# One hybrid decoder layer on one core: the token mixer's state scans, page use, weight splits and softmax scaling rearranged

## The chip, the cores and the metric

The kernel runs on one core of a Trainium2 chip, in one launch. The time is device microseconds (us) of one execution. The kernel before took 987.81 us in the median of three runs (985.87 to 990.09). The profiled execution took 985.9 us, of which 984.1 us are the span that the profile shows.

## The reference, cut to what matters

The input x is 512 tokens by 1024 channels, all float32. The layer is: a SwiGLU feed-forward block (width 2816), a token mixer, a second SwiGLU block, each with an RMS norm before and after it and a residual. The mixer projects the normed x to q, k, v (512 channels each) and u (512 channels), and computes two things that are concatenated and projected back:

```
# attention, 4 heads, two score maps c = 0, 1 a head (64 channels each), causal
p = softmax(q_c k_c^T / 8);  a = p[0] - lam * p[1];  o = rms_norm(a @ v, sub_g) * (1 - lam_init)
# state space, 32 groups of 16 channels, 64 complex states a group
state_t = a_bar * state_(t-1) + b_bar u_t;   y = Re(C state) + D u
g = gelu(y);  out = rms_norm(g * sigmoid(g @ w_glu + b_glu), norm_g)
```

## The kernel before, in words

**Matmul operands.** Almost every matmul is float32 by splitting: an operand is cast to a rounded high part (`wh`, `hi`) by ScalarE (ACT), and the rest (`wl`, `lo`) is the difference, taken by another engine; three products are added in PSUM (`mm3`, L182 to L184). `weights` (L160 to L177) loads 128x1024 values into `raw` (3 buffers), then splits them into `wh`, `wl` (4 buffers each), or into a heap page where `paged` is set. Which engine takes `wl` is the second argument of `split`: GpSimd (POOL) for paged weights, otherwise `lo_engine[0]`, which is VectorE (DVE) in the two feed-forward blocks and POOL from the start of the mixer to the last step of `fill`.

**Memory.** `page` hands out one of 15 heap pages of 128 x 2048 float32; `scratch` one of 6 buffers of 128 x 512; `bank` a PSUM bank by tag: four "acc", two "sc", two "m". A tile that finds no free buffer waits until an earlier one's last reader is done.

**Mixer, first part.** `out_block` of the first feed-forward block runs in two halves of 512 columns. Late in the second half a hook starts the next norm (`Normed`) and loads the four u weights (`ssm_lead`, paged). Then `ssm_load_states` requests the phase table `phases` and the input maps `im` (1 MB each transfer); `ssm_project` computes u (`ps_u`), writes it to DRAM as `ud` and reads it back regrouped as `u` in 16 small-packet transfers; `ssm_load_outputs` requests the output maps `om` and `mm` (2 and 16 transfers). `att_query(0)`, `att_key(0)`, four `ssm_states(blk)` and `att_values` follow.

**`ssm_states`.** For 8 groups a block: 16 fp32 matmuls into an "sc" bank (`ps_s`, L774); DVE multiplies it by cosines and by sines (L782, L783); POOL adds and subtracts (L785, L786); eight DVE scans of 64 steps with a per-partition decay (L791); products with cosines on DVE (L795) and with sines on POOL (L796); four DVE instructions combine them into `xt` (L802, L803), which stays in scratch until `ssm_outputs` reads it (`ps_y`, L813).

**Mixer, second part.** `attention` runs 16 score blocks (4 heads x 4 query tiles) in an order written out by hand for TensorE (PE) (`manual_schedule`); between them `pad` takes pieces of other PE work from `fill`: the q and k projections of heads 1 to 3, `ssm_outputs`, `glu`, the output projection. `att_scores` computes both maps into the two "sc" banks (`ps_sc`, L917 to L919), takes the row maximum on DVE (L921), the exponential with its row sum on ACT (L922), and on DVE the reciprocals times the coefficients (L924, L925), the scaling of map 0 (L926) and the combination (L927). `att_mix` transposes the result, copies it (L936) and multiplies by v (`ps_o`, L943). `att_norm` scales by the RMS norm and by `sub_g` (L954); `rsqrt_of` adds eps on DVE (L192) and takes the power on POOL (L193). `att_out` transposes and splits (L969, L970).

**Order.** Outside `manual_schedule` a planner orders every engine's instructions at build time by program order and by its own costs; on the chip each engine runs its list in that order.

Of the kernel before, what the change touches and what calls it, by code (L numbers as in the profile page):

```python
# [8 lines left out]
F32 = mybir.dt.float32  # L9
# [4 lines left out]
ALU = mybir.AluOpType  # L14
# [27 lines left out]
LO_ATT = 1  # L42
# [7 lines left out]
def hybrid_layer(  # L50
# [100 lines left out]
    lo_engine = [dve]  # L151
# [14 lines left out]
    def weights(src, shape, paged=False, late=None):  # L166
        raw = ring.tile(shape, F32, tag="raw", name="raw", bufs=3)
        if late is not None:
            pool.tensor_copy(raw[:, 0, 0:1], late)
        weights.dma = sp.dma_start(out=raw, in_=src).ins  # L170
        if paged:
            both = page([P, 2] + list(shape[1:]), F32R, "w_lead")
            wh, wl = both[:, 0], both[:, 1]
        else:
            wh = ring.tile(shape, F32R, tag="wh", name="wh")
            wl = ring.tile(shape, F32R, tag="wl", name="wl")
        with after(*behind):  # L177
            split(raw, wh, wl, pool if paged else lo_engine[0])
        return wh, wl
# [552 lines left out]
    def ssm_load_outputs():  # L732
        S.mm, S.om = [], []
        kd = S.kd.rearrange("(g h) s -> h g s", h=CH)
        for j in range(2):
# [16 lines left out]
    def ssm_project(xn, started, lead_w):  # L752
        units = [(bank("acc", "ps_u"), w) for w in lead_w]
        halves(units, xn, started)
        for j, (ps, _) in enumerate(units):
            ut = scratch([P, TC, NC], F32, "ut")
            act.copy(ut, ps.rearrange("p (c t) -> p t c", t=TC))
            act.dma_start(out=ud[j * P:(j + 1) * P, :], in_=ut.rearrange("p t c -> p (t c)"))
        S.u = page([P, GROUPS, NC], F32, "u")
        for hf in range(2):  # L760
            src = ud[hf * 256:(hf + 1) * 256, :].rearrange("(g h) (t c) -> t h g c", h=CH, t=TC)
            for tau in range(TC):
                sp.dma_start(out=S.u[tau * CH:(tau + 1) * CH, hf * 16:hf * 16 + 16, :], in_=src[tau])
        S.g = page([P, 4, SW], F32, "g")
        S.x = {}

    def ssm_states(blk):
# [12 lines left out]
        tcos = scratch([P, 2, 256], F32, "tcos")  # L780
        tsin = scratch([P, 2, 256], F32, "tsin")
        dve.tensor_tensor(tcos, pv, cos, ALU.mult)  # L782
        dve.tensor_tensor(tsin, pv, sin, ALU.mult)  # L783
        z = scratch([P, 2, 256], F32, "z")
        pool.tensor_tensor(z[:, 0], tcos[:, 0], tsin[:, 1], ALU.add)  # L785
        pool.tensor_tensor(z[:, 1], tcos[:, 1], tsin[:, 0], ALU.subtract)  # L786
        w = scratch([P, 2, 256], F32, "w")
        for ri in range(2):
            for g in range(4):
                cs = slice(g * NC, (g + 1) * NC)  # L790
                dve.tensor_tensor_scan(w[:, ri, cs], S.r8[:, blk * 4 + g:blk * 4 + g + 1].broadcast_to([P, NC]),  # L791
                                       z[:, ri, cs], 0.0, ALU.mult, ALU.add)
# [104 lines left out]
    def att_key(h, xn):  # L897

        A.k[h] = k = page([P, 3, SEQ], F32R, "k")
        ps = bank("acc", "ps_k2")  # L900
        yield from col_steps(ps, col_weights(w_in, 512 + h * P), xn, 0, SEQ)
        for c in range(2):
# [3 lines left out]
            dve.tensor_tensor(k[own, 2, :], ps[own], k[own, c, :].bitcast(F32), ALU.subtract)  # L906
        A.ready.add(h)

    def att_scores(h, i):
        q, k = A.q[h], A.k[h]  # L910
        A.pg[h, i] = pg = page([P, 4, SEQ], F32, "att")
        n = (i + 1) * P
        ssum = tiny(2, "psum", bufs=4)
        for c in range(2):
# [3 lines left out]
            pe.matmul(ps[:, 0:m], q[own, c, ts], k[own, 2, 0:m], start=False, stop=False)  # L918
# [4 lines left out]
        rc = tiny(2, "rc", bufs=4)  # L923
        dve.reciprocal(rc, ssum)  # L924
        dve.tensor_tensor(rc, rc, S.coef, ALU.mult)  # L925
        dve.tensor_scalar(pg[:, 0, 0:n], pg[:, 0, 0:n], rc[:, 0:1], None, ALU.mult)  # L926
        dve.scalar_tensor_tensor(pg[:, 0, 0:n], pg[:, 1, 0:n], rc[:, 1:2], pg[:, 0, 0:n], ALU.mult, ALU.add)  # L927

    def att_mix(h, i):
# [5 lines left out]
        at = pg[:, 2]  # L935
# [10 lines left out]
    def att_norm(h, i):  # L946
# [5 lines left out]
        ss = sum_sq(po, 1.0 / (VD ** 0.5), "att")  # L952
        r = rsqrt_of([ss], EPS, "att")
        dve.scalar_tensor_tensor(A.on[h][:, vs], po, r, A.sub, ALU.mult, ALU.mult)  # L954

    def att_out(h, blocks):
# [12 lines left out]
        act.copy(hi, A.pq[h][:, vs])  # L969
        dve.tensor_tensor(A.o[h // 2][:, h % 2, 1, vs], A.pq[h][:, vs], hi.bitcast(F32), ALU.subtract)  # L970
# [110 lines left out]

# [39 lines left out]
    lo_engine[0] = pool if LO_ATT else dve  # L1121
    with tc.manual_schedule(engines={mybir.EngineType.PE}):
# [3 lines left out]
        lo_engine[0] = dve  # L1126
# [43 lines left out]
```

## Time and profile before

| | |
|---|---|
| median of 3 runs | 987.81 us (985.87 to 990.09) |
| profiled execution | 985.9 us, span 984.1 us |
| PE busy | 963.3 us (98%) |
| DVE / ACT / POOL busy | 470.7 / 339.4 / 158.2 us |
| PE not busy, 430 to 480 us | 5.96 us of 50 |
| PE not busy, 480 to 620 us | 4.03 us of 140 |

PE is the engine that is almost always busy. [...]

### The profile page before, as it was taken

The page shows a single profiled execution, that of the slowest core. Times are in us where ns is not written, and L with a number is a line of the kernel's source. Part 1 is how long each engine was busy: PE and PEld are TensorE (multiplying, and loading weights), DVE is VectorE, ACT ScalarE, POOL GpSimd, SP SyncE. Part 2 cuts the span into 40 slices and gives each one's busy share as a digit, 9 for nine tenths or more (in the row PEclk, how much of TensorE's full clock was granted, in tenths as well). Part 3 has the DMA queues.
Part 4 walks back from the last instruction along what each step waited for, and adds up shares of the span by engine and source line. Part 5 has one row for each costly group of instructions (what it writes and reads, how often), then busy time and mean ns, then how long its engine had stood idle before and what let it go on. Part 6 is the DMA issues. An engine that isn't in the chain of part 4 may idle for free.

```text
span 984.1 us, 12804 instructions
## 1 busy us (share of the span) xinstructions
PE 963.3 (98%) x4956; PEld 792.7 (81%) x4956; DVE 470.7 (48%) x950; ACT 339.4 (34%) x568; POOL 158.2 (16%) x217
## 2 busy tenths in 40 slices
PE   9999999999999999998899899999999999999997
PEld 5988877788888888986677678988888888888886
DVE  5599877633322325447467656533333333412323
ACT  5423333323221334222676645422323232312211
POOL 2105333100000033236234315000000000000000
PEclk9999999999999999999899999999999999999999
DMA  6535543533323261697211215323333333232312
GB/s 202 168 92 150 168 132 110 153 97 96 104 90 106 87 190 41 238 184 144 65 44 44 86 43 151 107 65 99 95 103 90 104 88 107 86 107 86 107 43 86
DMA packets 146030, 107.18 MB, mean 109 GB/s; under 512 B 15553, under 2 KB 126689, under 8 KB 145202
## 3 DMA queue, kind: packets, MB, share of 16 engines
q1 hardware_dynamic: 143776, 100.93, 35.3%
q0 software_dynamic: 1040, 3.34, 1.0%
q10 hardware_dynamic: 1154, 2.10, 0.6%
q8 instruction: 39, 0.64, 0.3%
q14 instruction: 21, 0.17, 0.1%
HBM read 97.47 MB, written 8.88 MB: 108 GB/s over the span
## 4 chain that ended last, share of the span: by engine, by line
PE 48%; ACT 1%; DVE 1%; POOL 1%; issue 1%; DMA 0%; DVEq 0%; POOLq 0%; ACTq 0%
PE ps_gu L182 8%; PE ps_gu L183 8%; PE ps_gu L184 8%; PE acc L182 5%; PE acc L184 5%; PE acc L183 5%; PE ps_sc L918 1%; PE ps_o L943 1%; PE ps_sc L917 1%; PE ps_y L813 1%; PE ps_k L182 1%; PE ps_sc L919 1%; PE ps_k L183 0%; PE ps_q L182 0%; PE ps_k L184 0%
## 5 line engine op out<-in xcount | busy, mean ns | idle before, releaser
L155 ACT CAST wh<-raw 128x1024 fp32r<-128x1024 f32 x150 | 157.6, 1052 | 450.4 <-issue 156.8
L156 DVE TENSOR_TENSOR wl<-raw,wh 128x1024 fp32r<-128x1024 f32 x132 | 163.9, 1245 | 249.8 <-ACT wh L155 245.3
L182 PE MATMUL ps_gu<-xn_hi,wh 128*128 128x512 f32 (+1 forms) x696 | 265.6, 382 | 0.0
L183 PE MATMUL ps_gu<-xn_lo,wh 128*128 128x512 f32 (+1 forms) x696 | 265.5, 382 | 0.0
L184 PE MATMUL ps_gu<-xn_hi,wl 128*128 128x512 f32 (+1 forms) x696 | 265.3, 382 | 0.0
L182 PEld LDWEIGHTS ps_gu<-xn_hi,wh 128*128 128x128 f32 x696 | 130.8, 188 | 25.6 <-issue 0.8
L184 PEld LDWEIGHTS ps_gu<-xn_hi,wl 128*128 128x128 f32 x696 | 130.9, 188 | 25.0
L183 PEld LDWEIGHTS ps_gu<-xn_lo,wh 128*128 128x128 f32 x696 | 131.0, 188 | 24.2
L182 PE MATMUL acc<-wh,h 128*128 128x512 f32 x352 | 137.0, 390 | 0.0
L183 PE MATMUL acc<-wl,h 128*128 128x512 f32 x352 | 137.0, 390 | 0.0
L184 PE MATMUL acc<-wh,h 128*128 128x512 f32 x352 | 136.3, 390 | 0.0
L356 DVE TENSOR_TENSOR hf<-sg,ps_gu 128x512 f32<-128x512 f32 x44 | 30.2, 686 | 106.4 <-PE ps_gu L184 105.6
L184 PEld LDWEIGHTS acc<-wh,h 128*128 128x128 f32 x352 | 66.1, 188 | 13.8
L183 PEld LDWEIGHTS acc<-wl,h 128*128 128x128 f32 x352 | 66.1, 188 | 13.6
L182 PEld LDWEIGHTS acc<-wh,h 128*128 128x128 f32 x352 | 66.1, 188 | 13.6
L318 POOL TENSOR_SCALAR ss<-ss_post 128x1 f32<-128x1 f32 x12 | 2.6, 213 | 457.8 <-ACT junk_post L199 457.8
L156 POOL TENSOR_TENSOR wl<-raw,wh 128x1024 fp32r<-128x1024 f32 x18 | 44.3, 2464 | 53.7 <-ACT wh L155 53.6
L358 ACT CAST h<-hf 128x512 fp32r<-128x512 f32 x44 | 27.3, 621 | 37.7 <-DVE hf L356 31.2
L359 DVE TENSOR_TENSOR h<-hf,h 128x512 fp32r<-128x512 f32 x44 | 30.1, 685 | 1.4 <-ACT h L358 1.4
L199 ACT ACTIVATE junk_post<-acc 128x512 bf16<-128x512 f32 x24 | 14.3, 596 | 40.2 <-PE acc L184 40.0
L354 ACT ACTIVATE sg<-ps_gu 128x512 f32<-128x512 f32 x44 | 25.9, 588 | 1.5 <-PE ps_gu L184 1.5
L922 ACT ACTIVATE att<-ps_sc,mx 128x128 f32<-128x128 f32 (+3 forms) x32 | 16.8, 527 | 18.6 <-DVE mx L921 18.0
(292 smaller groups left out, 1227.6 us busy)
## 6 DMA issues: line engine op xcount, KB each, us to landing
raw<-in_ff_w_gate_dram SPq DMA_DIRECT2D x44, 512.0 KB, 3.9
raw<-in_ff_w_up_dram SPq DMA_DIRECT2D x44, 512.0 KB, 3.8
raw<-in_ff_w_down_dram SPq DMA_DIRECT2D x44, 512.0 KB, 3.3
raw<-in_w_in_dram SPq DMA_DIRECT2D x16, 512.0 KB, 3.9
raw<-in_w_out_dram SPq DMA_DIRECT2D x8, 512.0 KB, 3.3
im_d<-itca SPq DMA_DIRECT2D x4, 512.0 KB, 4.9
om_d<-taps SPq DMA_DIRECT2D x4, 512.0 KB, 4.5
im<-im_d SPq DMA_DIRECT2D x2, 1024.0 KB, 10.4
```

Source lines behind the costliest of these rows:

```text
L155: act.copy(wh, raw)
L156: eng.tensor_tensor(wl, raw, wh.bitcast(F32), ALU.subtract)
L182: pe.matmul(ps, a[0], b[0], start=start, stop=False)
L183: pe.matmul(ps, a[0], b[1], start=False, stop=False)
L184: pe.matmul(ps, a[1], b[0], start=False, stop=stop)
L199: sum_sq.ins = act.activation(into, src, AF.Square, scale=scale, accum_out=s).ins
L354: act.activation(sg, ps_g, AF.Silu)
L356: dve.tensor_tensor(hf, sg, ps_u, ALU.mult)
L358: act.copy(hi, hf)
L359: dve.tensor_tensor(lo, hf, hi.bitcast(F32), ALU.subtract)
L813: pe.matmul(ps[par * 64:par * 64 + 64, g * 64:(g + 1) * 64], lhs, rhs[:, g, par], start=(g == n == 0), stop=(g == 7 and n == 1), skip_grou ...
L922: act.activation(pg[:, c, 0:n], ps[:, 0:n], AF.Exp, bias=mx, accum_out=ssum[:, c:c + 1])
```

## The change

- Weight splits in the mixer: `lo_engine` is gone; weights that are not paged are split on DVE throughout. The splits of the first q and k weights are ordered behind the last norm's instructions (`behind`).
- `ssm_load_states` moves into the hook, behind `ssm_lead`; `ssm_load_outputs` is called for its first half ahead of `ssm_project` and for its second half after `att_values`.
- `ssm_states`: DVE does the adds, both products and the scans; a scan covers four groups at once, with a `decay` tile that POOL fills and whose first column of each group is zero. Results go to one page `states`.
- q and k of a head share one page; the low parts of k of all heads share one page `klo`; all attention maps share one page, two halves in turn.
- Attention: map 1 is combined into map 0 with the factor `ratio` = coefficient x sum0 / sum1; the division by sum0 is applied in `att_norm` instead. `sub_g` becomes a per-partition scale in `att_out`.
- `rsqrt_of` with one part adds eps on POOL.

```diff
-            split(raw, wh, wl, pool if paged else lo_engine[0])
+            split(raw, wh, wl, pool if paged else dve)
...
-            dve.tensor_scalar(r, parts[0], eps, None, ALU.add)
+            pool.tensor_scalar(r, parts[0], eps, None, ALU.add)
...
-        tcos = scratch([P, 2, 256], F32, "tcos")
...
-        pool.tensor_tensor(z[:, 0], tcos[:, 0], tsin[:, 1], ALU.add)
-        pool.tensor_tensor(z[:, 1], tcos[:, 1], tsin[:, 0], ALU.subtract)
+        zc = scratch([P, 2, 256], F32, "zc")
+        zs = scratch([P, 2, 256], F32, "zs")
+        decay = scratch([P, 4, NC], F32, "decay")
+        pool.tensor_copy(decay, S.r8[:, gs].unsqueeze(2).broadcast_to([P, 4, NC]))
+        pool.memset(decay[:, :, 0:1], 0.0)
+        dve.tensor_tensor(zc, pv, cos, ALU.mult)
+        dve.tensor_tensor(zs, pv, sin, ALU.mult)
+        dve.tensor_tensor(zc[:, 0], zc[:, 0], zs[:, 1], ALU.add)
+        dve.tensor_tensor(zc[:, 1], zc[:, 1], zs[:, 0], ALU.subtract)
         w = scratch([P, 2, 256], F32, "w")
         for ri in range(2):
-            for g in range(4):
...
-                dve.tensor_tensor_scan(w[:, ri, cs], S.r8[:, blk * 4 + g:blk * 4 + g + 1].broadcast_to([P, NC]),
-                                       z[:, ri, cs], 0.0, ALU.mult, ALU.add)
...
-        dve.tensor_tensor(wcos, w, cos, ALU.mult)
-        pool.tensor_tensor(wsin, w, sin, ALU.mult)
-        xt = scratch([P, 8, NC], F32, "xt")
-        pool.memset(xt[:, :, 0:1], 0.0)
+            dve.tensor_tensor_scan(w[:, ri], decay.rearrange("p g c -> p (g c)"), zc[:, ri], 0.0, ALU.mult, ALU.add)
+        dve.tensor_tensor(zc, w, cos, ALU.mult)
+        dve.tensor_tensor(zs, w, sin, ALU.mult)
+        if blk == 0:
+            S.xs = page([P, 4, 8, NC], F32, "states")
...
+        xt = S.xs[:, blk]
...
+        both = page([P, 4, SEQ], F32R, "qk")
+        A.q[h], A.k[h] = q, _ = both[:, 0:2], both[:, 2:4]
...
+            A.klo = page([P, HEADS, SEQ], F32R, "klo")
...
-        A.pg[h, i] = pg = page([P, 4, SEQ], F32, "att")
+            A.all = page([P, 4, SEQ], F32, "att")
...
-        dve.tensor_tensor(rc, rc, S.coef, ALU.mult)
-        dve.tensor_scalar(pg[:, 0, 0:n], pg[:, 0, 0:n], rc[:, 0:1], None, ALU.mult)
-        dve.scalar_tensor_tensor(pg[:, 0, 0:n], pg[:, 1, 0:n], rc[:, 1:2], pg[:, 0, 0:n], ALU.mult, ALU.add)
+        dve.scalar_tensor_tensor(ratio, rc[:, 1:2], ssum[:, 0:1], S.coef[:, 1:2], ALU.mult, ALU.mult)
+        dve.scalar_tensor_tensor(pg[:, 0, 0:n], pg[:, 1, 0:n], ratio, pg[:, 0, 0:n], ALU.mult, ALU.add)
+        pool.tensor_scalar(scale, rc[:, 0:1], 1.0 / (VD ** 0.5), None, ALU.mult)
...
-        dve.scalar_tensor_tensor(A.on[h][:, vs], po, r, A.sub, ALU.mult, ALU.mult)
+        dve.tensor_scalar(A.on[h][:, vs], po, r, rc, ALU.mult, ALU.mult)
...
-        act.copy(hi, A.pq[h][:, vs])
+        act.mul(hi, A.pq[h][:, vs], A.sub)
...
-    box, start, fin = next_norm(mix_pre_g, ssm_lead)
+    def mixer_lead():
+        lead = ssm_lead()
+        ssm_load_states()
+        return lead
+    box, start, fin = next_norm(mix_pre_g, mixer_lead)
...
-    lo_engine[0] = pool
-    ssm_load_states()
+    ssm_load_outputs(0)
     ssm_project(xn, started, box["w"])
-    ssm_load_outputs()
+    behind[:] = [xn.last_sq, xn.last]
     drain(att_query(0, xn))
     drain(att_key(0, xn))
+    behind.clear()
     for b in range(4):
         ssm_states(b)
     att_values(xn)
+    ssm_load_outputs(1)
```

## Rows read from the trace of the kernel before

**Rows 1.** Page, part 1: busy us, share of the span, instructions of each engine.

```profile
PE 963.3 (98%) x4956; PEld 792.7 (81%) x4956; DVE 470.7 (48%) x950; ACT 339.4 (34%) x568; POOL 158.2 (16%) x217
```

**Rows 2.** Busy time by stretch: start:end, length, each engine (instructions), clock, DMA share, GB/s.

```profile
430.00:480.00 50.00, 44.04 (x381) 34.26 (x378) 37.34 (x76) 18.21 (x30) 24.53 (x21) 0.90 0.68 126
480.00:620.00 140.00, 135.97 (x785) 106.18 (x782) 89.77 (x201) 85.96 (x208) 49.17 (x55) 0.99 0.23 72
620.00:900.00 280.00, 280.00 (x1319) 235.53 (x1318) 94.88 (x103) 80.75 (x103) 1.14 (x2) 1.00 0.32 96
...
460.00:466.00 6.00, 6.00 (x74) 4.62 (x74) 4.39 (x9) 0.49 (x1) 4.43 (x4) 0.72 0.32 92
...
471.10:478.00 6.90, 6.88 (x45) 4.88 (x45) 2.92 (x10) 5.78 (x10) 0.00 (x0) 0.51 0.17 50
```

**Rows 3.** PE's waits, 380 to 620 us: total us, times, longest.

```profile
PE ps_sc L917 <- DVE tsin L783: 3.1, 1, 3.1
...
PE ps_o L943 <- ACT o_ssm L862: 1.2, 1, 1.2
```

**Rows 4.** DVE in order of time, 430 to 471 us: start, us, instruction, idle before.

```profile
430.31 0.69 DVE L782 TENSOR_TENSOR tcos<-ps_s,phases 128x512 f32<-128x512 f32 x1 [22.15 <-PE ps_s L774]
430.92 0.68 DVE L783 TENSOR_TENSOR tsin<-ps_s,phases 128x512 f32<-128x512 f32 x1
...
433.78 1.58 DVE L791 TENSOR_TENSOR_SCAN w<-r,z 128x64 f32<-128x64 f32 x8
...
438.50 0.41 DVE L802 TENSOR_TENSOR xt<-wcos,wsin 64x252 f32<-64x252 f32 x1
...
466.91 2.48 DVE L803 TENSOR_TENSOR xt<-wcos,wsin 64x252 f32<-64x252 f32 x1
...
470.29 0.49 DVE L921 TENSOR_REDUCE mx<-ps_sc 128x1 f32<-128x128 f32 x2
```

**Rows 5.** POOL in order of time, 430 to 470 us.

```profile
430.16 2.39 POOL L156 TENSOR_TENSOR wl<-raw,wh 128x1024 fp32r<-128x1024 f32 x1 [3.05 <-ACT wh L155]
432.50 0.75 POOL L785 TENSOR_TENSOR z<-tcos,tsin 128x256 f32<-128x256 f32 x1
...
466.63 2.48 POOL L156 TENSOR_TENSOR wl<-raw,wh 128x1024 fp32r<-128x1024 f32 x1
```

**Rows 6.** Groups by form on DVE: instructions, total us, mean ns, idle before.

```profile
L156 DVE TENSOR_TENSOR wl<-raw,wh 128x1024 fp32r<-128x1024 f32 x132 | 163.9, 1245 | 249.8 <-ACT wh L155 245.3
L487 DVE TENSOR_TENSOR phases<-pslots 128x256 f32<-128x256 f32 x2 | 0.8, 412 | 0.0
```

**Rows 7.** PE in order of time at the two scores.

```profile
459.44 0.36 PE L917 MATMUL ps_sc<-k,q 128*128 128x256 f32 x1 [3.06 <-DVE tsin L783]
...
471.12 0.58 PE L917 MATMUL ps_sc<-k,q 128*128 128x256 f32 x1 [2.90 <-ACT att L922]
```

**Rows 8.** DVE groups by form in the attention stretch, 480 to 560 us.

```profile
L926 DVE TENSOR_SCALAR att<-att,rc 128x512 f32<-128x512 f32 x3 | 1.4, 483 | 0.1
...
L192 DVE TENSOR_SCALAR rinv_att<-ss_att 128x1 f32<-128x1 f32 x11 | 1.7, 150 | 0.1
```

**Rows 9.** POOL's splits in that stretch.

```profile
L156 POOL TENSOR_TENSOR wl<-raw,wh 128x1024 fp32r<-128x1024 f32 x8 | 19.7, 2465 | 27.7 <-ACT wh L155 27.7
```

**Rows 10.** DMA issues of the page: KB each, median us from issue to landing.

```profile
raw<-in_ff_w_down_dram SPq DMA_DIRECT2D x44, 512.0 KB, 3.3
...
im<-im_d SPq DMA_DIRECT2D x2, 1024.0 KB, 10.4
```

**Rows 11.** SP's queue in order of time.

```profile
353.32 8.50 SPq L170 DMA_DIRECT2D raw<-in_ff_w_down_dram  x4
```

**Rows 12.** ACT in order of time, 325 to 480 us.

```profile
369.23 1.05 ACT L155 CAST wh<-raw 128x1024 fp32r<-128x1024 f32 x1 [4.39 <-PE acc L184]
377.16 0.60 ACT L199 ACTIVATE junk_post<-acc 128x512 bf16<-128x512 f32 x1 [6.88 <-PE acc L184]
...
459.21 1.28 ACT L922 ACT_TABLE_LOAD   x1
```

More of the change, by code (lines that the diff above doesn't have):

```diff
@@ L730, in ssm_load_states, with ssm_load_outputs @@
             S.im += [t[:, 0], t[:, 1]]
-    def ssm_load_outputs():
-        S.mm, S.om = [], []
+    S.mm, S.om = [], []
+    def ssm_load_outputs(j):
         kd = S.kd.rearrange("(g h) s -> h g s", h=CH)
-        for j in range(2):
+        if True:
             t = page([P, 2, 1024], F32, "om")
@@ L763, in ssm_project @@
                 sp.dma_start(out=S.u[tau * CH:(tau + 1) * CH, hf * 16:hf * 16 + 16, :], in_=src[tau])
-        S.g = page([P, 4, SW], F32, "g")
         S.x = {}
@@ L801, in ssm_states @@
             rows = slice(two * 64, two * 64 + 64)
-            dve.tensor_tensor(xt[0:64, two::2, 1:NC], v(wcos, 0, rows), v(wsin, 1, rows), ALU.subtract)
-            dve.tensor_tensor(xt[64:128, two::2, 1:NC], v(wcos, 1, rows), v(wsin, 0, rows), ALU.add)
+            dve.tensor_tensor(xt[0:64, two::2, 1:NC], v(zc, 0, rows), v(zs, 1, rows), ALU.subtract)
+            dve.tensor_tensor(xt[64:128, two::2, 1:NC], v(zc, 1, rows), v(zs, 0, rows), ALU.add)
         S.x[blk] = xt
     def ssm_outputs(blk):
+        if blk == 0:
+            S.g = page([P, 4, SW], F32, "g")
         mm = S.mm[blk].rearrange("p (g i par h) -> p g par i h", g=8, i=4, par=2)
@@ L878, in att_values @@
         drain(row_steps(xn.get, w_in, KD, 1024, outer(KD, 2), keep_v))
-        A.sub = const.tile([P, VD], F32, name="subln")
+        A.sub = const.tile([P, 1], F32, name="subln")
         with after(*pool_behind):
-            pool.dma_start(out=A.sub, in_=attn_subln_g[0:1, :].broadcast_to([P, VD]))
-        with after(xn.lo_ins):
-            dve.tensor_scalar(A.sub, A.sub, 1.0 - LAM_INIT, None, ALU.mult)
+            pool.dma_start(out=A.sub, in_=attn_subln_g[0].rearrange("(p o) -> p o", o=1))
+            pool.tensor_scalar(A.sub, A.sub, 1.0 - LAM_INIT, None, ALU.mult)
         A.o, A.out = [], set()
     def att_query(h, xn):
-        A.q[h] = q = page([P, 2, SEQ], F32R, "q")
+        both = page([P, 4, SEQ], F32R, "qk")
+        A.q[h], A.k[h] = q, _ = both[:, 0:2], both[:, 2:4]
         ps = bank("acc", "ps_q")
@@ L897, in att_key @@
     def att_key(h, xn):
-        A.k[h] = k = page([P, 3, SEQ], F32R, "k")
+        k = A.k[h]
+        if h == 0:
+            A.klo = page([P, HEADS, SEQ], F32R, "klo")
         ps = bank("acc", "ps_k2")
@@ L905, in att_key @@
             act.copy(k[other, c, :], ps[own])
-            dve.tensor_tensor(k[own, 2, :], ps[own], k[own, c, :].bitcast(F32), ALU.subtract)
+            dve.tensor_tensor(A.klo[own, h, :], ps[own], k[own, c, :].bitcast(F32), ALU.subtract)
         A.ready.add(h)
@@ L910, in att_scores @@
         q, k = A.q[h], A.k[h]
-        A.pg[h, i] = pg = page([P, 4, SEQ], F32, "att")
+        if not A.pg:
+            A.all = page([P, 4, SEQ], F32, "att")
+        c0 = len(A.pg) % 2 * 2
+        A.pg[h, i] = pg = A.all[:, c0:c0 + 2]
         n = (i + 1) * P
@@ L917, in att_scores @@
             pe.matmul(ps[:, 0:m], q[:, c, ts], k[:, c, 0:m], start=True, stop=False)
-            pe.matmul(ps[:, 0:m], q[own, c, ts], k[own, 2, 0:m], start=False, stop=False)
+            pe.matmul(ps[:, 0:m], q[own, c, ts], A.klo[own, h, 0:m], start=False, stop=False)
             pe.matmul(ps[:, i * P:n], identb, cmask, start=False, stop=True)
@@ L934, in att_mix @@
             pe.transpose(pt[:, kb * P:(kb + 1) * P], pg[:, 0, kb * P:(kb + 1) * P], ident)
-        at = pg[:, 2]
+        at = pg[:, 1]
         act.copy(at[:, 0:n], pt[:, 0:n])
@@ L951, in att_norm @@
         po = A.po[h][:, vs]
-        ss = sum_sq(po, 1.0 / (VD ** 0.5), "att")
+        rc, scale = A.rc[h, i]
+        ss = sum_sq(po, scale, "att")
         r = rsqrt_of([ss], EPS, "att")
-        dve.scalar_tensor_tensor(A.on[h][:, vs], po, r, A.sub, ALU.mult, ALU.mult)
+        dve.tensor_scalar(A.on[h][:, vs], po, r, rc, ALU.mult, ALU.mult)
     def att_out(h, blocks):
```

23 lines of the change are left out of this document (8 added, 15 removed).

## The prediction

> **What bounds the kernel now.** Read the page's busy times first: PE is busy for 963.3 us of a span of 984.1 us, DVE for less than half of it [rows 1]. The change leaves every matmul of PE but for their order as it is, so it can give back only time in which PE waits or runs slowly, and take only by making PE wait. So the next view is busy time by stretch [rows 2]: from 620 to 900 us PE never pauses, from 430 to 480 us it lacks 5.96 us and from 480 to 620 us 4.03 us. The third view, PE's waits [rows 3], has the longest at its head: for the sines' product of the last state block (L783, DVE), which holds the "sc" bank that the first score needs. In order of time [rows 7] it runs from 456.4 to 459.4 us, and a second one, from 468.2 to 471.1 us, is for the first exponential (L922), which itself follows DVE's row maximum. [...] Work at those clocks loses (1 - 0.72) x 6 = 1.7 and (1 - 0.51) x 6.9 = 3.4 us. So this stretch holds 5.96 + 5.1 = 11.1 us that a faster state chain could return, and the chain is DVE's list from 430.31 us (the first product, which waited for `ps_s`) to 470.29 us, the first row maximum: 40.0 us [rows 4].
>
> **Why the chain takes 40 us.** DVE hands to POOL and back three times a block, and it is stretched where POOL does wide work: a combination (L803) took 2.48 us beside POOL's split of 2.48 us, where another of its shape (L802) takes 0.41 [rows 4, 5]. [...]
>
> **The change, part by part.**
>
> *State blocks.* On DVE a block then costs: two products from PSUM at 0.61 (430.31 to 430.92) = 1.22; two adds of 128x256, for which the nearest DVE row is 0.41 [rows 6], = 0.82; two scans of 256 columns; two products = 1.22; four combinations at 0.42 with their gap [rows 4] = 1.7. A scan of 256 columns isn't in the trace. It can't be below one of 64 (1.58 / 8 = 0.20 us), nor above four of them (0.79); I take the middle of the upper end and of the 128x256 add (0.41), 0.60, so 1.2 a block, ends 0.4 and 1.6. A block is 6.2 us (5.4 to 6.5), four are 24.7 (21.4 to 26.2). [...]
>
> *Other work in DVE's list.* Four low halves of q and k, as before; I charge them like the products of the same 512 columns, 0.68 each [rows 4], = 2.7 us. POOL ran five weight splits between 430.16 and 469.1 us, each about 2.4 us [rows 5]; on DVE one is 1.245 [rows 6]. Two of them (the last v weights, the next q weights) must come early, 2.5 us; the other three may stand before or behind: 6.2 us if all are ahead. The `decay` copies are new on POOL, 128x256 from SBUF, nearest row 0.75 [rows 5]. They depend on no data of the blocks and can run early; beside a two-input DVE instruction each could cost DVE its length, 0 to 3.0 us for four. [...] I take 1.
>
> *The two waits.* The last block's sines' product comes after three blocks and 1.2: 3 x 6.2 + 1.2 + 2.7 + 2.5 + 0.7 = 25.7 us after 430.3, at 456.0, against 459.3 before. PE needs it at 456.4, so the first wait is 0; with all splits ahead it is some 3, so I keep 0.6. DVE ends the blocks at 430.3 + 24.7 + 2.7 + 2.5 + 1 = 461.2 (464.9 with all five splits), against 470.29. PE comes to the second score at 468.2 - 3.06 (first wait gone) - 1.7 (clock) = 463.4, and the exponential was 0.8 us ahead of PE's start (470.29 to 471.12 [rows 4, 7]): 462.0 is in time, 465.7 would be 2.3 late; I keep 0.6. ACT is a second gate on the same exponential: its table load ended at 460.5 [rows 12], so it is also in time. With the waits go the slow clocks. For new small waits at full speed between 471 and 482 us I keep 0.4. Gain: 11.1 - 0.6 - 0.6 - 0.4 = 9.5 us.
>
> *Scratch and pages.* Before, each block's `xt` held one of six scratch buffers until `ssm_outputs`, so the last block's chain had few left. With one `states` page a block needs four and holds none. The heap gets lighter too: one page a head for q and k in place of two, one for all attention maps. I cost it at nothing; it is part of why the chain can run densely.
>
> *Attention, 480 to 560 us.* DVE loses the scaling of map 0, up to 0.48 us each (the widest form [rows 8]; 16 in all, some 6 us) and twenty eps additions at 0.15 [rows 8], 3.0 us; it gains eight splits at 1.245, 10.0 us, that POOL did in 19.7 [rows 9]. Net +1 us of DVE work over 80, with POOL out of its way: taken as 0. A split in front of a row maximum can add up to 1.25 us to one link of the attention chain; the 1.2 us wait for `o_ssm` [rows 3] is ACT's and stays. Ends: -4.0 (all waits of the stretch gone) to +3. The new POOL scalars (scale, eps) are 0.2 us off DVE's list and take the place of a hop between engines.
>
> *Norm of the mixer.* The first q and k splits move behind the last norm's square and scale and to DVE, 2.5 us there; PE has the whole projection of u to do before it needs them. Outside the two stretches PE lacks 984.1 - 963.3 - 5.96 - 4.03 = 10.8 us [rows 1, 2], the start and the tail among them, so little can be won back there. Nothing either way; without that cover a late split would cost PE up to its 1.245 us each.
>
> *`sub_g`.* POOL waits for the small transfer in its own list; what is queued behind it are the first `decay` copies, needed some 25 us later. Nothing.
>
> *Maps ahead of the inputs.* `phases`, `im` and half of `om`, `mm` leave SP's queue in the state stretch, where DMA is 0.68 busy [rows 2]. I charge PE no gain: what DVE waited for before its first product was PE's `ps_s` [rows 4], not a transfer. What they are moved past counts: in the hook stand also the last four down weights, issued from 353.32 over 8.5 us [rows 11], landing in 3.3 [rows 10], so by 365.1. Their last cast waited for a buffer until 369.23 and PE needs it, cast and split, six matmuls before the end of the first accumulator at 377.16 [rows 12], near 375.7. Slack: 4.1 + (375.7 - 369.23 - 1.05 - 1.23) = 8.3 us. One map of 1 MB in front costs between 2 x 3.3 = 6.6 (two loads of 512 KB) and 10.4 us [rows 10], so -1.7 to 2.1 late: no cost taken.
>
> Sum: 984.1 - 9.5 = 974.6 us of span; 1.8 us lie outside it (985.9), so 976.4. The profiled execution is 1.9 us under the median of the runs, so against the median: 978.3, told as 978.
>
> **The rivals.**
>
> *The chain stays long (half gain).* DVE puts all five splits and the slow ends of scan and copies in front: the last sines' product at 430.3 + 3 x 6.5 + 1.2 + 2.7 + 6.2 + 2.3 = 462.2, and the first wait is as long as now. For it: DVE has no room to spare in this stretch. Against: the planner has other places for three of the splits. The second wait then shrinks only by DVE's end, 470.3 to 468: about 5 us are kept, 983.
>
> [...]
>
> *It does not do what it says.* The planner orders every list anew, and another link (a page, ACT's table loads, the weights) is as late as DVE was: 988.
>
> *Slower: maps in front of the down weights.* If two maps are sent ahead of the last down weights, these land 20.8 us later, 12.5 past their slack; PE waits that long at 375 us and then loses 3.4 us of clock as after the wait at 471. Net +15.9 - 9.5 = +6.4: 994. It decides from 8.3 us of transfer ahead. For it: in program order the maps come before those weights. Against: the maps need pages that come free one after another as PE finishes the activations, and the down weights need none.
>
> **How the numbers follow.** Full gain 0.54 (978; its own range 975 to 981), gain with the attention waits 0.10 (974), half gain 0.17 (983), nothing 0.09 (988), slower 0.10 (994). The range 970 to 989 takes in all but the slower one and part of nothing. A measurement of this kernel tells 0.5%, 4.9 us, from no change, so faster means under 982.9: the first two and a third of the half gain, 0.70; the rest of that and nothing make same 0.19; slower 0.11.
>
> **What would show it.** The state stretch: no POOL instruction over 1 us between 420 and 470; a scan of 256 columns between 0.4 and 0.8 us; the first row maximum near 461 in place of 470.29; PE's two waits on `ps_sc` under 1 us each and a clock of 1.00 from 456 to 480. From 340 to 380 PE without a gap. It would be wrong if the maximum still comes after 468, if PE waits near 371 to 376 for down weights, or if new waits of over 3 us stand between 480 and 620.

## The result and the profile after

The kernel after took 974.59 us (971.8 to 975.95, 4 runs) against 986.84 us (985.47 to 990.09, 4 runs) of the kernel before on the same chip: ratio of the means 0.9868, 95% interval 0.9832 to 0.9904. The forecast was 978.0, range 970 to 989. The profiled execution took 971.8 us, its span is 970.0 us.

The page's busy line, which answers to [rows 1] (busy us, share, instructions):

```profile
PE 953.6 (98%) x4956; PEld 786.4 (81%) x4956; DVE 475.5 (49%) x919; ACT 342.4 (35%) x568; POOL 113.2 (12%) x229
```

Busy time by stretch of the kernel after, columns as in [rows 2]:

```profile
330.00:380.00 50.00, 50.00 (x222) 41.40 (x222) 15.88 (x17) 14.18 (x19) 11.27 (x7) 1.00 0.56 193
430.00:480.00 50.00, 50.00 (x490) 38.67 (x488) 37.21 (x71) 25.57 (x42) 4.37 (x13) 1.00 0.52 111
480.00:620.00 140.00, 134.70 (x736) 107.83 (x736) 95.47 (x175) 86.68 (x202) 36.12 (x76) 1.00 0.27 82
```

Between 430 and 480 us PE never pauses and never slows: 50.00 of 50 at a granted clock of 1.00, where it had 44.04 at 0.90. That is the whole 11.1 us that the stretch held. From 480 to 620 us it lacks 5.3 us in place of 4.03, but at clock 1.00 instead of 0.99.

Groups by tile, first the kernel before, then after (ns min/median/max, first and last start, form); the o_att rows are those of a window from 540 to 600 us, and only their first start is used:

```profile
L774 PE MATMUL ps_s<-u,im x128: 221/222/270, 429.1 to 442.2; 128*64 128x64 f32 x128
L182 PE MATMUL acc<-wh,o_att x21: 388/390/477, 571.5 to 599.5; 128*128 128x512 f32 x21
```

```profile
L772 PE MATMUL ps_s<-u,im x128: 222/222/270, 425.3 to 437.5; 128*64 128x64 f32 x128
L180 PE MATMUL acc<-wh,o_att x30: 389/389/481, 557.0 to 598.7; 128*128 128x512 f32 x30
```

From the first state matmul to the first output matmul on `o_att` before took 571.5 - 429.1 = 142.4 us, after 131.7: 10.7 us less. I call this length M below. From there to the end both take 412.6 to 413.0 us, and from the first matmul of the down projection to the first state matmul 158.0 and 158.5. So the mixer gave about 9.8 us net. The other 4.2 us of the 14.1 between the two spans lie in the first 15 us, which I call the head, in code that the change does not touch; PE in order of time, before and then after:

```profile
7.98 4.45 PE L121 MATMUL ps_warm<-zeros 128*128 128x512 bf16 x10
```

```profile
6.50 2.33 PE L120 MATMUL ps_warm<-zeros 128*128 128x512 bf16 x10
```

DVE's list of the state blocks after, shortened:

```profile
427.49 0.69 DVE L784 TENSOR_TENSOR zc<-ps_s,phases 128x512 f32<-128x512 f32 x1
...
429.29 0.41 DVE L786 TENSOR_TENSOR zc<-zc,zs 128x256 f32<-128x256 f32 x1
429.62 0.41 DVE L787 TENSOR_TENSOR zc<-zc,zs 128x256 f32<-128x256 f32 x1
429.96 0.68 DVE L790 TENSOR_TENSOR_SCAN w<-decay,zc 128x256 f32<-128x256 f32 x1
...
436.57 0.61 DVE L787 TENSOR_TENSOR zc<-zc,zs 128x256 f32<-128x256 f32 x1
...
446.20 1.19 DVE L154 TENSOR_TENSOR wl<-raw,wh 128x1024 fp32r<-128x1024 f32 x1
...
452.68 1.27 DVE L790 TENSOR_TENSOR_SCAN w<-decay,zc 128x256 f32<-128x256 f32 x2
...
457.04 0.49 DVE L926 TENSOR_REDUCE mx<-ps_sc 128x1 f32<-128x128 f32 x2
```

The first row maximum comes 29.6 us after the first product; before it was 40.0 [rows 4], the forecast 30.9. DVE is busy throughout, and three splits stand ahead of the maximum (438.89, 446.20 and 451.54). POOL does only the `decay` copies and small fills there:

```profile
436.26 0.65 POOL L782 COPY decay<-r 128x256 f32<-128x256 f32 x1 [20.43 <-DVE states L801]
```

PE's waits after, 420 to 620 us (total us, times, longest), the two longest; those of [rows 3] are gone:

```profile
PE ps_os L858 <- DVE qk L894: 2.0, 1, 2.0
PE ps_ot L973 <- DVE att_n L963: 0.8, 1, 0.8
```

SP's queue after, in order of time: the second half of the output maps now leaves behind the weights that the state stretch needs.

```profile
447.42 0.37 SPq L168 DMA_DIRECT2D raw<-in_w_in_dram  x1
448.51 6.34 SPq L741 DMA_DIRECT2D mm<-kd  x8
```

### The profile page after: what moved, and what is told of

Read it like the earlier page. It is cut to its first block, busy times and chain, and to the rows that moved or that the text cites. A ratio compares the mean times of both kernels' runs of the same rounds, so it can differ in the third digit from the quotient of the medians.

```text
span 970.0 us, 12795 instructions
## 1 busy us (share of the span) xinstructions
PE 953.6 (98%) x4956; PEld 786.4 (81%) x4956; DVE 475.5 (49%) x919; ACT 342.4 (35%) x568; POOL 113.2 (12%) x229
## 4 chain that ended last, share of the span: by engine, by line
PE 75%; DVE 5%; DMA 2%; issue 2%; ACT 1%; POOL 1%; SPq 0%; DVEq 0%; POOLq 0%; ACTq 0%
PE ps_gu L180 12%; PE ps_gu L181 11%; PE ps_gu L182 11%; PE acc L180 9%; PE acc L182 9%; PE acc L181 9%; PE ps_sc L923 1%; PE ps_o L951 1%; PE ps_y L813 1%; PE ps_u L181 1%; PE ps_u L182 1%; PE ps_q L180 1%; PE ps_u L180 1%; DVE wl L154 1%; PE ps_q L182 1%
## 5 line engine op out<-in xcount | busy, mean ns | idle before, releaser
L154 DVE TENSOR_TENSOR wl<-raw,wh 128x1024 fp32r<-128x1024 f32 x150 | 185.9, 1242 | 275.7 <-ACT wh L153 252.8
L181 PEld LDWEIGHTS ps_gu<-xn_lo,wh 128*128 128x128 f32 x696 | 130.9, 188 | 24.4
L356 ACT CAST h<-hf 128x512 fp32r<-128x512 f32 x44 | 27.4, 622 | 37.3 <-DVE hf L354 30.9
L154 POOL TENSOR_TENSOR w_lead<-raw,w_lead 128x1024 fp32r<-128x1024 f32 x8 | 19.6, 2457 | 21.1 <-ACT w_lead L153 21.1
L926 DVE TENSOR_REDUCE mx<-ps_sc 128x1 f32<-128x128 f32 (+3 forms) x32 | 15.4, 488 | 13.4 <-PE ps_sc L924 13.4
```

The lines of the kernel that those rows point to most:

```text
L181: pe.matmul(ps, a[0], b[1], start=False, stop=False)
L356: act.copy(hi, hf)
L926: dve.tensor_reduce(mx, ps[:, 0:n], AX.X, ALU.max, negate=True)
```

## The experiments

One table first. PE and clock are busy time and mean granted clock of a stretch; M is worked out for each kernel as above. The kernel before, run beside them, had medians of 986.71 (16 runs, with a1 to a4), 988.04 (30, with a5 and b1 to b3) and 987.93 us (7, with the rest); each ratio is against its own.

| kernel | us (runs) | ratio to before, 95% | PE, clock 430-480 | PE, clock 480-620 | M |
|---|---|---|---|---|---|
| before | 986.84 (4) | | 44.04, 0.90 | 135.97, 0.99 | 142.4 |
| after | 974.59 (4) | 0.9832 to 0.9904 | 50.00, 1.00 | 134.70, 1.00 | 131.7 |
| a1_repeat | 976.49 (1) | | 50.00, 1.00 | 134.96, 0.99 | 133.2 |
| a2_splits_pool | 985.91 (10) | 0.9977 to 1.0018 | 47.25, 0.97 | 136.05, 1.00 | 135.3 |
| a3_states_pool | 982.42 (7) | 0.9932 to 0.9973 | 47.18, 0.97 | 135.39, 0.98 | 138.7 |
| a4_scans8 | 974.49 (4) | 0.9839 to 0.9917 | 50.00, 1.00 | 134.78, 0.99 | 133.0 |
| a5_maps_late | 980.23 (10) | 0.9893 to 0.9949 | 47.34, 0.97 | 134.63, 0.99 | 137.7 |
| a6_second_half | 973.44 (4) | 0.983 to 0.9878 | 50.00, 1.00 | 134.96, 0.99 | 132.8 |
| a7_softmax_old | 977.15 (4) | 0.9872 to 0.9922 | 50.00, 1.00 | 133.96, 0.98 | 135.9 |
| a8_wout_pool | 972.76 (4) | 0.9826 to 0.9868 | 50.00, 1.00 | 135.54, 1.00 | 130.9 |
| b1_states_alone | 985.63 (10) | 0.995 to 0.9988 | 46.16, 0.93 | 134.92, 0.99 | 139.7 |
| b2_splits_alone | 982.39 (10) | 0.9928 to 0.9973 | 46.73, 0.97 | 133.23, 0.99 | 140.3 |
| b3_states_and_splits | 983.83 (9) | 0.9937 to 0.9992 | 47.88, 0.97 | 133.44, 0.99 | 139.1 |
| b4_states_splits_half | 978.40 (4) | 0.9886 to 0.9925 | 50.00, 1.00 | 133.94, 0.99 | 133.9 |

**a1_repeat**: the kernel after, unchanged.

> The changed kernel again, unaltered, for one more profile. Of the 14.1 us by which the two profiled spans differ (984.1 and 970.0), 4.2 stand before 15 us, in code that the change does not touch (ten warming matmuls took 4.45 us before and 2.33 after). If that is chance, this span is either near 970 or near 974, and from the first ps_s matmul (425.3) to the first product of w_out with o_att (557.0) it is 131.7 us within 0.5. If it belongs to the change, the ten warming matmuls take 2.3 us in every run of it.

Measured: 976.49 us; in the head a warming matmul took 634 ns in the median, as before, against 379 in the profile of after, so the 4.2 us there are chance and no part of the change. PE in a1:

```profile
7.98 4.39 PE L120 MATMUL ps_warm<-zeros 128*128 128x512 bf16 x10
```

M was 133.2, 1.5 us more than expected: the lengths of a stretch repeat to about that, and smaller differences of M are not read below.

**a2_splits_pool**: the kernel after, but the splits of unpaged mixer weights on POOL again.

```diff
-            split(raw, wh, wl, pool if paged else dve)
+            split(raw, wh, wl, pool if paged else lo_engine[0])
...
+    lo_engine[0] = pool
     ssm_load_outputs(0)
...
+        lo_engine[0] = dve
         started = next(box["b"])
```

> The changed kernel with the mixer's unpaged weight splits back on POOL. My theory (the gain is that DVE's list of the state stretch got shorter and is no longer blocked by wide POOL work): five splits of about 2.4 us block two-input DVE instructions, DVE saves 5 x 1.24 and loses up to 5 x 2.4, so the first row maximum comes up to 6 us later than 457.0, PE waits 0 to 3 us at the scores and the time rises by 1 to 7 us (976 to 982). Rival (the gain came from the emptier transfer queue): same as the changed kernel, 974.6. In the attention stretch both expect the 2.0 us wait of ps_os to go.

Measured: no gain left at all, more than the theory asked. More than half of it goes in a place that the prediction had costed at nothing, the mixer's norm. Busy time of a2:

```profile
380.00:430.00 50.00, 45.57 (x299) 41.72 (x299) 24.81 (x32) 18.20 (x38) 14.93 (x15) 0.97 0.48 119
430.00:480.00 50.00, 47.25 (x440) 37.08 (x440) 39.01 (x62) 20.33 (x32) 17.02 (x16) 0.97 0.53 114
```

In the first stretch after has 49.22 at 1.00. What DVE and POOL do there in a2, and then the same DVE instruction in after:

```profile
398.44 8.84 DVE L218 SCALAR_TENSOR_TENSOR xs<-x,rinv_pre,pre_g 128x512 f32<-128x512 f32 x2 [0.66 <-POOL rinv_pre L192]
```

```profile
399.01 7.04 POOL L155 TENSOR_TENSOR wl<-raw,wh 128x1024 fp32r<-128x1024 f32 x3
```

```profile
394.46 1.41 DVE L217 SCALAR_TENSOR_TENSOR xs<-x,rinv_pre,pre_g 128x512 f32<-128x512 f32 x2 [0.66 <-POOL rinv_pre L191]
```

Two scalings of 1.41 us together took 8.84 while three splits ran back to back on POOL, and PE waited 3.6 us for them. The 7.4 us more are about the length of all three splits (7.04), so at least one of the two scalings lost more than one split's 2.3 us. In the state stretch of a2 the same meeting hits a scan, 0.68 us long in after (DVE, then POOL):

```profile
446.10 2.88 DVE L791 TENSOR_TENSOR_SCAN w<-decay,zc 128x256 f32<-128x256 f32 x1
```

```profile
446.05 2.38 POOL L155 TENSOR_TENSOR wl<-raw,wh 128x1024 fp32r<-128x1024 f32 x1
```

Three such scans (2.88, 2.89 and 2.45) and a combination of 2.59 put the first row maximum at 471.25. From the down projection to the first state matmul a2 takes 164.0 us, 5.5 more than after, and M is 3.6 longer. The wait on `ps_os` is gone, as expected.

**a3_states_pool**: the kernel after, but the two adds and the sines' product of each block on POOL.

```diff
-        dve.tensor_tensor(zc[:, 0], zc[:, 0], zs[:, 1], ALU.add)
-        dve.tensor_tensor(zc[:, 1], zc[:, 1], zs[:, 0], ALU.subtract)
+        pool.tensor_tensor(zc[:, 0], zc[:, 0], zs[:, 1], ALU.add)
+        pool.tensor_tensor(zc[:, 1], zc[:, 1], zs[:, 0], ALU.subtract)
...
-        dve.tensor_tensor(zs, w, sin, ALU.mult)
+        pool.tensor_tensor(zs, w, sin, ALU.mult)
```

> The changed kernel with the two adds and the sines' product of each state block back on POOL, in place, splits still on DVE. My theory: a block hands over to POOL and back; three POOL instructions take 0.75 + 0.75 + 1.3 to 1.7 where DVE took 0.34 + 0.34 + 0.6, so the last row maximum comes 4 to 8 us after 457.0, the scores wait again (1 to 5 us) with a slow clock behind it, and the time rises by 3 to 9 us (978 to 984). Rival (queue): 974.6, no change. Rival (scratch buffers): no change either, since no buffer is added.

Measured: 7.8 us over after, inside what was expected, but not where. From the first state matmul to the first maximum it took 33.4 us against 31.7, only 1.7 more. The larger loss is behind it: SP's queue and PE at 468 us.

```profile
428.01 18.53 SPq L168 DMA_DIRECT2D raw<-in_ssm_w_glu_dram  x2
454.33 7.08 SPq L741 DMA_DIRECT2D mm<-kd  x8
```

```profile
468.39 0.34 PE L813 MATMUL ps_y<-mm,u 128*64 128x64 f32 x4 [1.88 <-ACT qk L893]
```

SP stood 18.5 us on two weights of the GLU (13.0 in after), probably for buffers, so `mm` left 5.8 us later than in after (454.33 against 448.51), and PE's `ps_y`, which reads `mm`, stopped. The row names ACT; that it was `mm` in truth is read from the times, since these transfers take a median of 8.8 us to land in a3. The granted clock of 468 to 472 us was then 0.59. Slow clocks of 0.62 from 536 to 540 and 0.75 from 552 to 556 us add to the loss. The planner lays out every list anew for each kernel, so an edit of three instructions can also have moved this; what moved it is not shown.

**a4_scans8**: the kernel after with eight scans of 64 columns a block and no `decay`.

```diff
-        decay = scratch([P, 4, NC], F32, "decay")
-        pool.tensor_copy(decay, S.r8[:, gs].unsqueeze(2).broadcast_to([P, 4, NC]))
-        pool.memset(decay[:, :, 0:1], 0.0)
...
-            dve.tensor_tensor_scan(w[:, ri], decay.rearrange("p g c -> p (g c)"), zc[:, ri], 0.0, ALU.mult, ALU.add)
+            for g in range(4):
+                cs = slice(g * NC, (g + 1) * NC)
+                dve.tensor_tensor_scan(w[:, ri, cs], S.r8[:, blk * 4 + g:blk * 4 + g + 1].broadcast_to([P, NC]),
+                                       zc[:, ri, cs], 0.0, ALU.mult, ALU.add)
```

> The changed kernel with eight scans of 64 a block in place of two of 256, and no decay tile. My theory: 4 x (1.58 - 1.27) = 1.2 us more on DVE, less four POOL copies of 0.4 to 0.65; the row maximum comes at 457 to 459, PE's wait at the scores stays under 1 us, and the time is the same within 1.5 us (973 to 976.5). If the two long scans were a main part of the gain, the time rises by 3 us or more.

Measured: 974.49, as after. Four short scans in a4:

```profile
434.46 0.82 DVE L788 TENSOR_TENSOR_SCAN w<-r,zc 128x64 f32<-128x64 f32 x4
```

0.82 against 0.68 us, eight times: 1.1 us of DVE's list, and PE still has 50.00 of 50 between 430 and 480 us.

**b1_states_alone, b2_splits_alone, b3_states_and_splits**: the kernel before with the new `ssm_states`, with the splits on DVE, and with both. The first takes over the function as the diff of the change has it; the second is this:

```diff
-    lo_engine[0] = pool
     ssm_load_states()
...
-    lo_engine[0] = pool if LO_ATT else dve
```

> The kernel before with the new ssm_states alone (two scans, no wide POOL work in it, states page); weight splits stay on POOL, maps, pages and softmax as before. If the handing over between DVE and POOL inside a block made the 40 us, DVE's list shrinks to 32 us or less and most of the gain shows: 977 to 981. If POOL's weight splits made it, as the run with the splits back on POOL says (985.9), the list stays over 36 us and the time is 983 to 987.

> The kernel before with the weight splits on DVE alone; ssm_states with its POOL work and eight scans, maps, pages and softmax as before. If POOL's splits were the cause, nothing of 2.4 us blocks DVE any more, but POOL's share of a block stays in the chain: first row maximum 32 to 37 us after the first sines' product in place of 39.4, time 979 to 984. If the splits on DVE only lengthen its list, the time is 987 or more.

> The kernel before with the new ssm_states and with the splits on DVE; maps, page sharing, softmax and eps on POOL as before. My theory: these two carry the gain; time 974 to 978, DVE's list near 30 us, no wait over 1 us at the first two scores. Rival (the map requests moved ahead, or the lighter heap, carry a part): 980 to 985, with a wait for a transfer or for a page in the state stretch.

Measured: 985.63, 982.39 and 983.83. From the first product to the first row maximum DVE takes 36.2, 35.9 and 33.1 us, against 40.0 before and 29.6 after. The first two came out inside what was expected if POOL's splits make the length. The third is the miss of this study: the two edits that I took for the whole gain bring, by their ratios, a quarter and two fifths of it, and together no more than the larger alone. The reason stands in three lists of b3, SP, ACT and DVE:

```profile
432.32 9.18 SPq L742 DMA_DIRECT2D mm<-kd  x8
442.30 0.40 SPq L170 DMA_DIRECT2D raw<-in_w_in_dram  x1
```

```profile
451.93 1.05 ACT L155 CAST wh<-raw 128x1024 fp32r<-128x1024 f32 x1 [10.59 <-DMA raw<-in_w_in_dram]
```

```profile
453.01 1.23 DVE L156 TENSOR_TENSOR wl<-raw,wh 128x1024 fp32r<-128x1024 f32 x1 [3.39 <-ACT wh L155]
```

Eight requests for `mm`, of 128 KB each, hold SP for 9.2 us (the one for a weight of 512 KB takes 0.40), the weight behind them arrives for the cast at 451.93, and its split, which now stands in DVE's list, holds up the state blocks behind it for 3.4 us. In before that weight is as late, but its split stands in POOL's list, where POOL was idle 0.74 us for it.

**a5_maps_late**: the kernel after with all map requests where before had them.

```diff
-        ssm_load_states()
         return lead
...
-    ssm_load_outputs(0)
+    ssm_load_states()
     ssm_project(xn, started, box["w"])
+    ssm_load_outputs(0)
+    ssm_load_outputs(1)
...
     att_values(xn)
-    ssm_load_outputs(1)
```

> The changed kernel with the map requests where they were before: phases and im after the first feed-forward block, both halves of om and mm right after the projection of u. My theory: no gain from them, 973 to 977. Rival (queue): u and the weights of the state stretch arrive later behind 2 MB of small packets, ACT waits for them, and 2 to 6 us are lost (977 to 981); the run with the states on POOL, where PE waited 1.9 us at ps_y while SP still sent mm, speaks for some effect.

Measured: 980.23, 5.6 us over after. My theory of that moment was wrong and the queue's rival right. DVE of a5 stops as in b3:

```profile
453.06 1.22 DVE L154 TENSOR_TENSOR wl<-raw,wh 128x1024 fp32r<-128x1024 f32 x1 [3.91 <-ACT wh L153]
```

**a6_second_half**: as a5, but the second half of the output maps stays behind `att_values`.

```diff
+    ssm_load_states()
     ssm_project(xn, started, box["w"])
+    ssm_load_outputs(0)
...
     att_values(xn)
     ssm_load_outputs(1)
```

> The kernel after with phases, im and the first half of the output maps requested where they were before (behind the hook, and behind ssm_project); only the second half stays behind att_values. Theory (what cost 5.7 us with all maps late is the second half's small packets in front of the k and glu weights, on whose split DVE's list then stands): 974 to 977, the first row maximum by 459, no DVE idle of over 1 us between 445 and 456. Rival (all the early requests are needed): 979 to 982, with a DVE stop before a split as with all maps late.

Measured: 973.44, as after; of the moves of the maps only this one counts. Its queue, in which the weight leaves at 432.92 us (442.30 in b3), and the cast that stands at the same place of ACT's list as the late one of b3:

```profile
432.92 0.39 SPq L168 DMA_DIRECT2D raw<-in_w_in_dram  x1
450.34 0.37 SPq L168 DMA_DIRECT2D raw<-in_w_in_dram  x1
451.43 6.85 SPq L741 DMA_DIRECT2D mm<-kd  x8
```

```profile
444.03 1.06 ACT L153 CAST wh<-raw 128x1024 fp32r<-128x1024 f32 x1 [4.56 <-PE acc L182]
```

The cast waits for PE's `acc` and for no transfer. DVE has no stop of over 1 us between 445 and 456 us. Its first maximum comes at 460.0, 31.8 us after its first state matmul at 428.2, as in after (31.7); the expected "by 459" forgot that the head can shift everything by 4 us.

**b4_states_splits_half**: b3 with the second half of the output maps behind `att_values`.

```diff
-    ssm_load_outputs()
+    ssm_load_outputs(0)
...
     att_values(xn)
+    ssm_load_outputs(1)
```

> The kernel before with three edits: the new ssm_states, all unpaged splits on DVE, and the second half of the output maps requested behind att_values. Theory (these three in series are the whole gain): 975 to 979, against the 983.8 of the first two alone, with the DVE stop of 3.4 us before the split gone and the first row maximum near 459. Rival (page sharing, the norm's ordering and the first maps matter as well): 980 to 983, with another wait in the stop's place.

Measured: 978.40; PE has 50.00 of 50 at 1.00 between 430 and 480 us, and DVE's stop is gone. The third edit takes b3's M from 139.1 to 133.9. In the state stretch these three are the whole gain. What is left to after lies behind 480 us, where b4 has 133.94 at 0.99, and is small in the traces: the span of b4 is 975.6 us, that of a1, which has the same long head, 974.7. The medians differ by 3.8 us; how much of that is the head is not shown.

**a7_softmax_old**: the kernel after with the row sum divided out ahead of the values again.

```diff
-        dve.scalar_tensor_tensor(ratio, rc[:, 1:2], ssum[:, 0:1], S.coef[:, 1:2], ALU.mult, ALU.mult)
-        dve.scalar_tensor_tensor(pg[:, 0, 0:n], pg[:, 1, 0:n], ratio, pg[:, 0, 0:n], ALU.mult, ALU.add)
+        dve.tensor_tensor(rc[:, 0:2], rc[:, 0:2], S.coef, ALU.mult)
+        dve.tensor_scalar(pg[:, 0, 0:n], pg[:, 0, 0:n], rc[:, 0:1], None, ALU.mult)
+        dve.scalar_tensor_tensor(pg[:, 0, 0:n], pg[:, 1, 0:n], rc[:, 1:2], pg[:, 0, 0:n], ALU.mult, ALU.add)
...
-        dve.tensor_scalar(A.on[h][:, vs], po, r, rc, ALU.mult, ALU.mult)
+        dve.tensor_scalar(A.on[h][:, vs], po, r, None, ALU.mult)
```

> The kernel after with the division by the row sums in front of the combination again (one more wide DVE instruction a score block; sub_g and eps stay as after). Theory (attention moves nothing, as forecast): within 1.5 us of after, 973 to 976.5. Rival (DVE, which has no idle time between 525 and 536, is a bound there): 977 to 980, and PE's wait of 2.0 us on ps_os grows to 3 or more.

Measured: 977.15, just outside the first and just inside the second. Busy time of a7 at the wait on `ps_os`, and behind it:

```profile
530.00:536.00 6.00, 3.37 (x15) 2.53 (x14) 5.90 (x13) 4.33 (x13) 1.76 (x5) 0.83 0.33 105
536.00:540.00 4.00, 4.00 (x19) 2.70 (x18) 2.80 (x6) 1.78 (x7) 1.38 (x3) 0.83 0.02 7
```

The wait is 2.6 us, not 3, but two stretches of slow clock follow (0.83 here, 0.63 from 548 to 552 us), where after has 1.00 in each. But a1, which is the same kernel as after, also slows down there:

```profile
548.00:552.00 4.00, 4.00 (x12) 3.01 (x13) 1.34 (x5) 0.46 (x2) 0.79 (x2) 0.57 0.03 8
```

So the slow clock can't be put down to the softmax. The interval of a7's ratio overlaps that of after, and the size, some 3 us, is not certain.

**a8_wout_pool**: the kernel after with only the output projection's splits on POOL.

```diff
+        lo_engine[0] = pool
         box["b"] = out_block(mixed
...
+        lo_engine[0] = dve
         started = next(box["b"])
```

> The kernel after with only the splits of the output projection's weights, made inside the attention stretch, on POOL. Theory (two such splits on DVE make PE's wait of 2.0 us on ps_os, but POOL's hold of 2.4 us each costs about as much elsewhere): 973 to 976. Rival (the wait was pure loss): 971 to 973, ps_os wait gone and nothing in its place. Third: a hold falls on a row maximum: 976 to 979.

Measured: 972.76, in the rival's range by its time, while another wait came, as the theory asked; by its interval it is not to be told from after. DVE of after, and PE at the wait:

```profile
525.75 1.22 DVE L154 TENSOR_TENSOR wl<-raw,wh 128x1024 fp32r<-128x1024 f32 x1
527.00 0.69 DVE L894 SCALAR_TENSOR_TENSOR qk<-ps_q,qk 64x512 fp32r<-64x512 f32 x1
527.71 1.23 DVE L154 TENSOR_TENSOR wl<-raw,wh 128x1024 fp32r<-128x1024 f32 x1
```

```profile
532.00 0.63 PE L858 MATMUL ps_os<-ident,og 128*128 128x128 f32 x4 [1.98 <-DVE qk L894]
```

With these splits on POOL that wait is gone, and another of 1.5 us takes most of its place in a8:

```profile
PE ps_o L952 <- DVE att_n L964: 2.0, 2, 1.5
```

It is the best median here, but no version was found that is measurably faster than after.

## Why the prediction was right, and where it was not

**State blocks: right.** The scan was set at 0.60 us and is issued 0.60 apart (two in 1.27, one alone 0.68); adds 0.41, products and combinations as read from [rows 4, 6]. Taking the two low halves (0.7 each) and the three splits (1.2) out of the 29.6 us leaves 24.5 for four blocks, against 24.7 and 1 for the copies. The other work in the list came out at the forecast's size by luck: two low halves in place of four (1.4 us against 2.7), three splits in place of two (3.6 against 2.5). A fourth split ends just ahead of the first product, which so starts 2.2 us behind the first state matmul in place of 1.2. In after it is 0.60 us from scan to scan and 0.33 from add to add of the same width. The longer scan cost nothing that shows: a4 has 1.1 us more of scans and the same time.

**The two waits: right in place, a little low in size.** 9.5 us were taken of 11.1, and all 11.1 came. The 0.6, 0.6 and 0.4 kept back were not needed: DVE's list was 1.3 us shorter than forecast, and ACT's table load came at 453.54, before 459.21 [rows 12]. The 1.7 and 3.4 us of slow clock in the sum are worked out from the granted clocks 0.72 and 0.51 of [rows 2]; in windows of 2 us before has 0.50 from 462 to 464 and from 472 to 476 us, while after has 1.00 all through 430 to 480 us.

**`decay` copies.** Two copies of 0.65 us stand beside DVE's adds (436.26 and 443.57), and there an add takes 0.61 and 0.62 in place of 0.41. So a copy costs about 0.2 us where 0.25 was charged, and not its whole length.

**Norm of the mixer: right in sum, wrong in meaning.** It was costed at nothing either way, and before and after are nearly equal there (49.76 and 49.22 of 50). But a2 shows that, with the new order of lists, leaving the splits on POOL would cost this stretch about 5 us (45.57 at 0.97). The edit is needed so that the others don't lose.

**Maps: the step that failed.** "I charge PE no gain" argued from what DVE waited for before its first product. That was the wrong DVE wait. With the splits in DVE's list, a late weight became a stop of the state chain (3.4 us in b3, 3.9 in a5), and the second half of the output maps made that weight late: 5.6 us in a5, 5.2 us of M between b3 and b4. The total stood only because the forecast took for granted that DVE's list would run without a stop. The queue was also misread: in before `phases` and `im` left SP ahead of the state stretch, and what stood in it were `om` and `mm`, in front of a weight for whose transfer ACT then waited (SP, SP, ACT of before):

```profile
391.52 0.90 SPq L729 DMA_DIRECT2D im<-im_d  x2
434.22 9.75 SPq L742 DMA_DIRECT2D mm<-kd  x8
453.77 1.05 ACT L155 CAST wh<-raw 128x1024 fp32r<-128x1024 f32 x1 [12.89 <-DMA raw<-in_w_in_dram]
```

The requests ahead of the inputs brought nothing to M (132.8 in a6 without them, 133.2 in a1) and cost about 1 us ahead of it: from the down projection to the first state matmul a5 and a6 take 157.2 and 157.3 us, after and a1 158.5. That they do not delay the down weights was right in its result, with PE at 50.00 of 50 from 330 to 380 us, but by luck. The maps did not have to wait behind those weights: in after all three go ahead of three of the last four (SP, then ACT):

```profile
349.67 0.46 SPq L723 DMA_DIRECT2D phases<-cs_d  x1
350.18 0.90 SPq L727 DMA_DIRECT2D im<-im_d  x2
351.57 6.12 SPq L168 DMA_DIRECT2D raw<-in_ff_w_down_dram  x3
367.02 1.06 ACT L153 CAST wh<-raw 128x1024 fp32r<-128x1024 f32 x1 [0.24 <-DMA raw<-in_ff_w_down_dram]
```

So the order that the slower rival feared did come, and its price did not: the last four down weights took a median of 9.6 us to land in place of 4.4, and with the head's 4.2 us added back the last cast came at 371.2 against 369.23, 2.0 us later, where the rival reckoned with 20.8.

**Pages: not tested apart.** The page `states` came with the new `ssm_states` in every run. The other shared pages, the `behind` order and eps on POOL are missing in b4, so the state stretch does not need them.

**Attention: right as a sum of two terms.** It was costed at nothing, -4 to +3. The 4 us that the forecast's 974 counts on did not come: PE lacks 5.3 us in after, 4.03 before. By PE's busy time of 480 to 620 us, with one trace of each kernel, there are four cases: splits on POOL with the long softmax 135.97 and 134.92 (before, b1), with the short one 136.05 (a2); splits on DVE with the long one 133.23 to 133.96 (b2, b3, b4, a7), with the short one 134.63 to 135.39 (after, a1, a3 to a6). So the splits cost some 1 to 2 us and the softmax gives some 1 back, while equal cases differ by up to 1 us. What the clock adds is not shown, as a1 beside after tells. The new wait on `ps_os` follows the splits: 2.0 to 2.6 us in every trace with these splits on DVE, none with them on POOL (before, b1, a2, a8). It is the price that was named as "up to 1.25 us to one link", two splits long.

**The signs named in advance.** POOL has no instruction over 1 us in the stretch, the scan lies between 0.4 and 0.8, PE's waits on `ps_sc` are under 1 us, and the new wait of 2.0 us is below the 3 that would have spoken against the forecast. The first maximum stands at 457.04; with the 4.2 us of the head added back that is 461.2, the forecast's number, but partly by luck: the list was 1.3 us shorter than forecast and started 1.4 us later.

**The total.** 9.8 us of net mixer gain in this pair of profiles, 8.5 with a1 in the place of after, against 9.5 forecast. The near hit is in part luck: the stretch gave back 1.6 us more than was charged (11.1), and 1.3 us that were costed at nothing were lost, 0.5 ahead of the first state matmul, 0.4 behind it within M and 0.4 at the end. The remaining 2.5 us of the measured 12.3 can be the head, whose 4.2 us fall by chance: it is short in four of the fourteen profiles (after, a3, a7, b2). How it fell in the runs without a profile is not known, so this part is argued and not shown.

## What to carry to other kernels

In b3 and a5 DVE, which took over the splits, took over their waits too (3.4 and 3.9 us): before moving a split onto the engine of the critical chain, look which transfer feeds it and what stands ahead of that transfer in the queue. Parts of a change can be gates in series: here two alone gave a quarter and two fifths, both together no more, and a third, a reordered request, released most of the rest; judge such parts by taking one out of the whole as well as by adding one alone. Read the stage, not only the total: busy time and clock of 430 to 480 us put the variants in two groups (50.00 at 1.00, or under 48) where run times overlap, as those of a5 (973.36 to 983.84) and after (971.8 to 975.95) do.

## What the runs showed of the hardware that was not expected

Two DVE instructions beside POOL's splits lost more than two splits' length: they took 8.84 us for 1.41 us of work beside three splits of 7.04 us together (a2). The warming matmuls of the head took 379 or 634 ns in the median in executions of the same kernel (after and a1), with a granted clock of 1.00 from 4 to 12.2 us both times; what decides it stays open. The clock behind the short waits of the attention differs between two executions of the same kernel: from 548 to 552 us it is 1.00 in after and 0.57 in a1, which is about 1.7 us of work ((1 - 0.57) x 4, an estimate).
